# Values' upper columns as a token-major Strassen step ahead of queries and keys

## The chip, the cores and the metric

The kernel runs on one core of a Trainium2 chip. The core has a matmul engine (PE, with its weight loads shown apart as PEld), a vector engine (DVE), a scalar engine (ACT), a general engine (POOL), and a queue engine (SP) that issues nearly all DMAs in this kernel. Matmuls write to PSUM, which has eight banks of 128 partitions by 512 float32 numbers; DVE and ACT read PSUM, POOL can't. Everything else lies in SBUF, with 128 partitions. The metric is device time in microseconds of one execution, as the median of several runs.

## The reference

A block of a language model on 1024 tokens of width 1024, all in float32. Eight attention heads with a forgetting gate (512 columns) and eight groups of a gated mixing over chunks of 128 tokens (512 columns) are computed side by side from one input projection, and joined by an output projection. Then follows a gated feed-forward part of width 2816 with a short convolution. The parts that matter here:

```python
def chunked_spatial_gating(u, vg, v_gain, w_s, b_s):
    ...
    vg = rmsnorm(vg, v_gain.reshape(G, Dg))
    vc = vg.reshape(B, nc, CHUNK, G, Dg)
    w = w_s * jnp.tril(jnp.ones((CHUNK, CHUNK), dtype=w_s.dtype))
    mixed = jnp.einsum('gij,bnjgd->bnigd', w, vc) + b_s.T[None, None, :, :, None]
    return (u * mixed.reshape(B, S, G, Dg)).reshape(B, S, G * Dg)

def reference(...):
        ...
        xn = rmsnorm(h, norm_mix_g[layer])
        proj = xn @ w_in[layer]
        q = proj[..., :Q_END].reshape(B, S, N_ATT_HEADS, ATT_HEAD_DIM)
        k = proj[..., Q_END:K_END].reshape(B, S, N_ATT_HEADS, ATT_HEAD_DIM)
        v = proj[..., K_END:V_END].reshape(B, S, N_ATT_HEADS, ATT_HEAD_DIM)
        log_f = jax.nn.log_sigmoid(
            (proj[..., G_END:] + b_forget[layer]).astype(jnp.float32))
        att = forgetting_attention(q, k, v, log_f)
        uv = jax.nn.gelu(proj[..., V_END:G_END])
        ...
        sg = chunked_spatial_gating(u, vg, gmlp_norm_g[layer], w_spatial[layer], b_spatial[layer])
        mix = jnp.concatenate([att, sg], axis=-1)
        h = h + mix @ w_out[layer]
        h = h + conv_ffn(rmsnorm(h, norm_ffn_g[layer]), w_up[layer], conv_w[layer],
                         conv_b[layer], w_down[layer])
    return rmsnorm(h, norm_final_g)
```

## The kernel before

**Precision.** Each float32 operand is split into a high part and a low part of a shorter float format (`fp32r`): ACT casts the high part, DVE subtracts it from the source (`split_w`, L151). A product is then three matmuls: high by high, high by low, low by high.

**Strassen.** Large products are cut in two along the tokens, the contraction and the columns, and done with seven block products instead of eight. The blocks of x are called B11, B21, B22 and T1 to T4 (sums and differences), those of the weights A11, A12, A22 and S1 to S4. The class `Weights` (L434) loads a set, `sums` and `last_sum` form S1 to S4 on POOL, and `split` makes the two parts. `product` (L425) is one feature-major block product: 4 blocks of the contraction by 3 terms, 12 matmuls, with a block of 128 weight columns stationary and 512 tokens moving. `tmul` (L259) is token-major: a block of 128 tokens of x is stationary, and the weight's columns move; one call does 4 token blocks by 3 terms for one block of the contraction.

**Order of the stages.** First the two gate halves (u and vg), then the values' lower 256 columns together with the forget gate's 8 columns (`values_low`, `values_high`, L485, 264 moving columns). Then the queries and keys in four steps (`qk_step`, L594). A step computes 128 columns of q and of k at once, two heads of each, in seven products; `emit` (L570) scales by the norm (`rb`, the inverse root mean squares of all tokens laid along a row), splits and stores them to DRAM. Between the products the next step's weights are loaded and split (`nxt_of`, L579), and the forget gate's running sums are formed (`forget_sums`, L534), whose negative goes to DRAM, comes back, is split on POOL and stored once more (L798 to L854).

After the last step come the values' upper 256 columns, in token-major form with 256 moving columns: four products of 48 matmuls each, against T3, B11, B21 and B22, into two PSUM banks that hold 256 columns of two token blocks each (L803 to L847). This is the eight-product form, with one sum of weights on POOL (L815). `evac_v` (L684) scales the values by the norm and splits them into the tiles `V`; `kept` (L696) does this for the lower columns, which were kept in DRAM. During this stage the gate's gain and splits are also done, and head 0's operands are loaded (`head_loads`, L823). Then come the mixing (`spatial`, L744: 8 groups of three matmuls of 512 columns, bias and multiplication by u on DVE, ACT and POOL) and the turning of the gated tiles (`turn_sg`, L775, 32 transposes). Then attention starts: logits of head 0 for the row blocks 7 down to 0 (`logits_mm`, L914; `logits_min`, L924, adds the causal mask `msk` and takes the row minimum; `logits_exp`, L941), with two PSUM places for two row blocks.

**Attention** runs 40 steps of one list, 5 for each head: turning of the probabilities, products with the values, and the logits of the next head. The output projection of the gated tiles is cut in 16 pieces (`sg_out`, L996) that fill PE's waits at places that `FILLS` (L21) names.

**The end** is the down projection, also in Strassen form (`dprod`, L1529). Its last product, A22, updates the last four token blocks; each is then squared, normalized and stored (`finish`, L1606).

**What sets the order.** The program is written once, and a planner at build time orders each engine's instructions by their place in the text and by when it takes them to be ready; it also gives out the buffers, so an instruction can pass another that isn't ready. Places where it must not are tied by hand: `after` puts one instruction behind another, `seq` (L710) chains PE in attention, `behind` and `gates` hold back side work, and `act.on` and `dve.on` keep an engine in the text's order. SP executes its DMAs in order. Buffers have tags with counts (`BUFS`): for instance 4 of `raw` (loaded weights), 4 of `whl` and 2 of `wy` (split weights), 3 of `pt`, 4 each of `G`, `H` and `V`, 2 of `A`.

## Time and profile before

| what | us |
|---|---|
| median of three runs | 1055.32 |
| lowest, highest | 1055.31, 1055.50 |
| the profiled execution | 1055.89 |
| its span, first to last instruction | 1054.2 |
| end of the last query and key product | about 183.3 |
| first matmul of the mixing | 206.6 |
| first matmul of attention's logits | 215.6 |

The granted clock of PE is 0.999 over the span. A row of the timeline or of a group gives the engine, the line of the kernel, the operation, the tiles written and read, the shape, and the count. In the busy time of PE a matmul's end is modelled and lies beyond the start of the next, so a pace is read from starts. Idle time before an instruction, and what ended it, stands in brackets.

### The profile page before, as it was taken

To read this page: it belongs to the slowest core of one execution; us is meant where nothing else is said; L and a number is where in the kernel's file an instruction comes from. 1 tells how busy PE (TensorE), PEld (TensorE's weight loads), DVE (VectorE), ACT (ScalarE), POOL (GpSimd) and SP (SyncE) were. 2 spreads that over 40 slices of the span, in tenths; PEclk is the share of its full clock that TensorE was granted. 3 is DMA by queue.
4 is the path that set the end of the run, shared out by engine and by line. 5 is a ranking of instruction groups with operands and counts; after the bars stand their busy time and mean duration, and the time that the engine had idled before them with its cause. 6 is when DMAs were issued, how large, how long until landed. Compare 5 with 4: busy or idle time off the path is not lost.

```text
span 1054.2 us, 14328 instructions
## 1 busy us (share of the span) xinstructions
PE 1043.7 (99%) x5028; PEld 874.0 (83%) x5028; DVE 883.1 (84%) x1291; ACT 568.4 (54%) x1005; POOL 234.7 (22%) x177
## 2 busy tenths in 40 slices
PE   9999999999999999999999999999999999999997
PEld 7988888988888888888888888888888888888886
DVE  6898787777787769998999989899897866897774
ACT  6777544557766736654444444444444554454653
POOL 0003241420420740253333423323331000000000
PEclk9999999999999999999999999999999999999999
DMA  9623465756655444222255332331322999333442
GB/s 313 222 16 135 125 167 164 218 163 183 186 155 160 159 161 161 80 82 99 81 179 170 120 109 82 130 120 67 131 84 80 309 325 313 103 99 100 146 119 95
DMA packets 67471, 155.77 MB, mean 148 GB/s; under 512 B 9060, under 2 KB 10036, under 8 KB 67400
## 3 DMA queue, kind: packets, MB, share of 16 engines
q1 hardware_dynamic: 66088, 154.82, 46.6%
q8 instruction: 39, 0.64, 0.3%
q14 instruction: 32, 0.26, 0.1%
q10 hardware_dynamic: 1312, 0.04, 0.1%
HBM read 111.96 MB, written 42.87 MB: 147 GB/s over the span
## 4 chain that ended last, share of the span: by engine, by line
PE 90%; DVE 4%; DMA 2%; ACT 2%; issue 1%; SPq 0%; ACTq 0%; DVEq 0%
PE k L1546 20%; PE qc L1288 11%; PE qa L1288 11%; PE qd L1288 11%; PE qb L1288 5%; PE ps L265 4%; PE pb L984 3%; PE pb L968 2%; PE pb L265 2%; PE qa L430 2%; PE qc L430 2%; PE qd L430 2%; PE pl L920 1%; PE pl L921 1%; PE pf L1008 1%; PE pf L1009 1%
## 5 line engine op out<-in xcount | busy, mean ns | idle before, releaser
L1546 PE MATMUL k<-whb,wha 128*128 128x512 f32 x924 | 209.7, 389 | 0.0
L1546 PEld LDWEIGHTS k<-whb,wha 128*128 128x128 f32 x924 | 173.3, 188 | 36.2 <-DVE wha L161 0.2
L1288 PE MATMUL qc<-xT,whb 128*128 128x512 f32 x540 | 129.8, 389 | 0.2 <-ACT whb L155 0.2
L1288 PE MATMUL qa<-xB,wha 128*128 128x512 f32 x528 | 127.4, 390 | 0.0
L1288 PEld LDWEIGHTS qc<-xT,whb 128*128 128x128 f32 x540 | 101.3, 188 | 21.6 <-ACT whb L155 0.6
L1288 PEld LDWEIGHTS qa<-xB,wha 128*128 128x128 f32 x528 | 98.8, 188 | 20.9 <-DVE wha L161 0.4
L155 ACT CAST wha<-sg 128x512 fp32r<-128x512 f32 x77 | 47.8, 622 | 96.9 <-PE k L1546 84.4
L155 ACT CAST whb<-sg 128x512 fp32r<-128x512 f32 x82 | 50.5, 618 | 87.7 <-PE qc L1288 67.5
L161 DVE TENSOR_TENSOR wha<-sg,wha 128x512 fp32r<-128x512 f32 x77 | 52.8, 688 | 39.5 <-ACT wha L155 39.4
L1288 PE MATMUL qd<-xB,whb 128*128 128x512 f32 x264 | 63.7, 389 | 0.0
L1288 PE MATMUL qd<-xT,whb 128*128 128x512 f32 x264 | 63.7, 389 | 0.0
L969 ACT CAST pt<-pb 128x512 fp32r<-128x512 f32 x72 | 40.5, 585 | 41.5 <-PE pb L968 36.1
L1172 POOL TENSOR_TENSOR sg<-raw 128x512 f32<-128x512 f32 x20 | 31.1, 1555 | 139.1 <-DVE whb L161 79.9
L1288 PE MATMUL qb<-xT,whb 128*128 128x512 f32 x252 | 61.0, 389 | 0.0
L161 DVE TENSOR_TENSOR whb<-sg,whb 128x512 fp32r<-128x512 f32 x82 | 57.0, 697 | 4.4 <-ACT whb L155 4.3
L970 DVE TENSOR_TENSOR pt<-pb,pt 128x512 fp32r<-128x512 f32 x72 | 47.9, 688 | 15.1 <-ACT pt L969 14.9
L1288 PEld LDWEIGHTS qd<-xT,whb 128*128 128x128 f32 x264 | 49.5, 188 | 10.5 <-DVE u L1395 0.3
L1288 PEld LDWEIGHTS qd<-xB,whb 128*128 128x128 f32 x264 | 49.6, 188 | 10.3
L1288 PEld LDWEIGHTS qb<-xT,whb 128*128 128x128 f32 x252 | 47.2, 188 | 10.0 <-DVE whb L161 0.3
L984 PE MATMUL pb<-pt,V 128*128 128x512 f32 (+3 forms) x192 | 49.6, 362 | 0.4 <-DVE pt L970 0.3
L1175 POOL TENSOR_TENSOR sg<-sg,raw 128x512 f32<-128x512 f32 x20 | 33.4, 1672 | 63.3 <-DVE whb L161 63.3
L1173 POOL TENSOR_TENSOR sg<-sg,raw 128x512 f32<-128x512 f32 x20 | 35.1, 1754 | 47.2 <-issue 44.6
(412 smaller groups left out, 2269.8 us busy)
## 6 DMA issues: line engine op xcount, KB each, us to landing
raw<-wup SPq DMA_DIRECT2D x44, 512.0 KB
sg<-hx SPq DMA_DIRECT2D x77, 256.0 KB
hx<-hs SPq DMA_DIRECT2D x44, 256.0 KB
hx<-ca SPq DMA_DIRECT2D x35, 256.0 KB
xT<-wdn SPq DMA_DIRECT2D x28, 256.0 KB
x<-kd SPq DMA_DIRECT2D x24, 256.0 KB
A<-xtok SPq DMA_DIRECT2D x8, 512.0 KB
raw<-wqk SPq DMA_DIRECT2D x8, 512.0 KB
```

Of the source, the lines that this page charges most:

```text
L155: act.copy(h, src)
L161: return eng.tensor_tensor(out=l, in0=src, in1=f32(h), op=ALU.subtract)
L265: pe.matmul(banks[m], xs(n, xi, k)[:, ms], w[:, wi, :], start=(first and k == 0 and c == 0 and (own or m % 2 == 0)), stop=(k == 3 and c == ...
L430: pe.matmul(ps, w[:, wi, ks], xs(n, xi, k), start=(first and c == 0), stop=(c == 11), skip_group_check=True)
L969: casts.append(act.copy(pt[:, 0, :], ptr))
L970: los.append(dve.tensor_tensor(out=pt[:, 1, :], in0=ptr, in1=f32(pt[:, 0, :]), op=ALU.subtract))
L984: seq(pe.matmul(po[half][:, o:o + w], lhs, pt[:, s, c:c + w], start=(new and s == 0), stop=(s == 1 and (half, k) in ((1, 6), (0, 3))), ski ...
L1172: pool.tensor_tensor(out=s[0], in0=a21, in1=a22, op=ALU.add)
L1173: pool.tensor_tensor(out=s[1], in0=s[0], in1=a11, op=ALU.add)
L1175: pool.tensor_tensor(out=s[3], in0=s[1], in1=a12, op=ALU.add)
L1288: pe.matmul(ps, w[:, wi, ks], xb[:, xi, k, :], start=(first and n == 0), stop=(n == 11), skip_group_check=True)
L1546: pe.matmul(banks[bk + m], xh[:, xi, ms], wh[:, wi, :], start=(first and p_ == 0 and n == 0), stop=(p_ == NP - 1 and n == 2), skip_group_c ...
```

## The change

The values' upper columns are done before the queries and keys, as one Strassen step with a set of weights of its own (`Weights(4)`, the values' columns laid out like those of a step). Its seven products are token-major (`vproduct`): a block of 128 tokens is stationary, 128 weight columns move, and the four token blocks of a PSUM bank are done in turn. The four result blocks are combined on DVE and stored to a DRAM tensor `vu`. They come back into one tile when attention is at its third step, and are scaled and split in the steps 5 to 12, one token block in each.

The gate's gain and splits move in among these products, and so do the spatial weights and the forget gate's sums, whose negative is now split at once, without the round trip. Mixing follows the first product of step 0 of the queries and keys. Its low part lies in other tiles, so one matmul of 512 columns becomes two of 256. The gated tiles are turned inside the steps 1 to 3. In step 3 the tiles for q, k and two of the weights are taken from other tags; the first output weights and head 0 are loaded there, and the lower values of the first half are scaled and split there. Attention then starts right after step 3 and `kept(1)`. The mask is written into the buffer of `rb`. Of the places of `FILLS` one moves from head 0's first step to the start. Three warming matmuls at the start go, the first product is done by pairs of token blocks, and the last product of the end is cut for its last token block at column 320, into a bank of its own, so that its parts are squared apart.

```diff
 NFF = 22
-WARM = 11
-
-FILLS = {(-1, j): 1 for j in (5, 3, 2)} | {(h, s): 1 for h in range(6) for s in ((0, 2, 4) if h == 0 else (2, 4))}
+WARM = 8
+
+FILLS = {(-1, j): 1 for j in (5, 3, 2, 0)} | {(h, s): 1 for h in range(6) for s in (2, 4)}
 FCFG = ("b", 4, 4)
...
-        for m, c in sorted(ops, key=lambda o: (o[1] > 0, o)) if apart else ops:
+        for m, c in sorted(ops, key=lambda o: (o[0] // 2, o[1])) if apart else ops:
...
     values_high(1)
-    W = [Weights(0)]
-    W[0].split("A11")
+    wv = Weights(4)
+    wv.split("A11")
     values_high(2)
-    W[0].split("A12")
-    W[0].sums()
-    W[0].last_sum()
+    wv.split("A12")
+    wv.sums()
+    wv.last_sum()
     values_high(3)
     gates["high"] = newest[0]
...
     gate_norm()
+    gain = sb("pt", [P, 512])
+    sp.dma_start(out=gain, in_=ggain.to_broadcast((P, 512)))
     xu = {}
+
+    def vproduct(ps, w, n, first):
+        for k in range(4):
+            for c, (xi, wi) in enumerate(((0, 0), (0, 1), (1, 0))):
+                for m in range(4):
+                    ms = slice(m * P, (m + 1) * P)
+                    pe.matmul(ps[:, ms], xs(n, xi, k)[:, ms], w[:, wi, k * P:(k + 1) * P],
+                              start=(first and k == 0 and c == 0 and m == 0), stop=(k == 3 and c == 2),
+                              skip_group_check=True)
 
     def q1(i, tag):
         qa = psq(tag)
...
         act.copy(xu[i][:, 0, :], qa)
         return qa
-
-    qa = q1(0, "a")
-    q2 = psq("a")
-    product(q2, W[0].w["A12"], "B21", True)
 
     def forget():
 
...
-        sp.dma_start(out=ncr.rearrange("h (t p) -> (h t) p", p=P), in_=rows)
+        pool.tensor_copy(hi_, rows)
+        pool.tensor_tensor(out=lo_.bitcast(F32R), in0=rows, in1=f32(hi_), op=ALU.subtract)
+        for n, t in ((0, f32(hi_)), (1, lo_)):
+            sp.dma_start(out=ncd[n].rearrange("h (t p) -> (h t) p", p=P), in_=t)
         yield
 
+    def gate_gain(hf):
+        for t in (0, 2):
+            v = vgt[hf][:, t:t + 2, :]
+            dve.tensor_tensor(out=v, in0=v, in1=gain.unsqueeze(1).to_broadcast((P, 2, 512)), op=ALU.mult)
...
+    def gate_split(hf, gh):
+
+        if vgh[gh] is None:
+            vgh[gh] = sb("G", [P, 4, 8, 64], F32R)
+        if hf:
+            l = lw[gh]
+        else:
+            if gh == 0:
+                vgl[0] = sb("G", [P, 8, 4, 64], F32R)
+            l = vgl[0][:, gh * 4:gh * 4 + 4]
+        src = vgt[hf][:, :, gh * 256:(gh + 1) * 256].rearrange("p t (g d) -> p g t d", g=4)
+        h = vgh[gh][:, :, hf * 4:hf * 4 + 4, :]
+        act.copy(h, src)
+        dve.tensor_tensor(out=l, in0=src, in1=f32(h), op=ALU.subtract)
...
+    def spatial():
+
+        tmp = [sb("raw", [P, 4, 256]) for _ in range(2)]
+        v3 = lambda t: t.rearrange("p (t d) -> p t d", d=64)
+        for g in range(8):
+            ps = bank()
+            gs = slice(g * 64, (g + 1) * 64)
+            vh_ = vgh[g // 4][:, g % 4]
+            pe.matmul(ps, ws[0][:, g, :], vh_, start=True, stop=False)
+            for hf, vl_ in ((0, vgl[0][:, g]), (1, lw[g // 4][:, g % 4])):
+                pe.matmul(ps[:, hf * 256:hf * 256 + 256], ws[0][:, g, :], vl_,
+                          start=False, stop=False, skip_group_check=True)
+            pe.matmul(ps, ws[1][:, g, :], vh_, start=False, stop=True)
+            u = [ut[hf][:, :, gs] for hf in range(2)]
+            dve.scalar_tensor_tensor(out=u[0], in0=v3(ps[:, 0:256]), scalar=bs[:, g:g + 1], in1=u[0],
+                                     op0=ALU.add, op1=ALU.mult)
+            t = tmp[g // 4][:, g % 4, :]
+            act.activation(t, ps[:, 256:512], AF.Identity, bias=bs[:, g:g + 1])
+            pool.tensor_tensor(out=u[1], in0=v3(t), in1=u[1], op=ALU.mult)
...
+    va, v2 = psq("a"), psq("a")
+    vproduct(va, wv.w["A11"], "B11", True)
+    vx = sb("pt", [P, 2, 512])
+    x1, u2 = vx[:, 0, :], vx[:, 1, :]
+    act.copy(x1, va)
+    vproduct(v2, wv.w["A12"], "B21", True)
+    wv.split("S2", "S3")
     fg = forget()
+    fsum = forget_sums(*fg)
+    next(fsum)
+    gate_gain(1)
+    next(fsum)
+    gate_gain(0)
+    ws = spatial_weights()
+    rtags[0] = ("whl",) * 4
+    lw = [sb("wy", [P, 4, 4, 64], F32R) for _ in range(2)]
+    wv.split("S1")
+    W = [Weights(0)]
+    vb = psq("b")
+    vproduct(vb, wv.w["S2"], "T2", True)
+    dve.tensor_tensor(out=u2, in0=vb, in1=x1, op=ALU.subtract)
+    wv.split("A22")
+    vc = psq("c")
+    vproduct(vc, wv.w["S3"], "T3", True)
+    vr = ring(F32)
+    r22, r12 = vr[:, 0, :], vr[:, 1, :]
+    dve.tensor_tensor(out=r22, in0=u2, in1=vc, op=ALU.add)
+    gate_split(1, 0)
+    gate_split(1, 1)
+    vd_ = psq("d")
+    vproduct(vd_, wv.w["S1"], "T1", True)
+    next(fsum)
+    dve.tensor_tensor(out=r22, in0=r22, in1=vd_, op=ALU.subtract)
+    dve.tensor_tensor(out=x1, in0=v2, in1=x1, op=ALU.add)
+    W[0].split("A11")
+    wv.split("S4")
+    gate_split(0, 0)
+    vproduct(vc, wv.w["A22"], "T4", False)
+    dve.tensor_tensor(out=r12, in0=u2, in1=vc, op=ALU.add)
+    gate_split(0, 1)
+    W[0].split("A12")
+    W[0].sums()
+    W[0].last_sum()
+    vproduct(vd_, wv.w["S4"], "B22", False)
+    dve.tensor_tensor(out=u2, in0=vd_, in1=u2, op=ALU.subtract)
+    for r_, h_, f_ in ((x1, 0, 0), (r12, 0, 1), (u2, 1, 0), (r22, 1, 1)):
+        sp.dma_start(out=vu[4 * h_:4 * h_ + 4, :, f_ * P:(f_ + 1) * P].rearrange("m p f -> p m f"),
+                     in_=r_.rearrange("p (m f) -> p m f", f=P))
+    qa = q1(0, "a")
+    next(fsum)
+    spatial()
+    rtags[0] = RTAG
+    q2 = psq("a")
+    product(q2, W[0].w["A12"], "B21", True)
+    W[0].split("S2", "S3")
...
+        tq_, tk_ = global_ if i < 3 else (sb("H", [P, 2, 1024]), sb("H", [P, 2, 1024]))
...
+            late_w = sb("V", [P, 2, 2, 512], F32R)
+
+            def wsplit(n, j):
+                w.w[n] = late_w[:, j]
+                split_w(w.src[n], (late_w[:, j, 0], late_w[:, j, 1]))
+        else:
+            def wsplit(n, j):
+                w.split(n)
+        wsplit("S1", 0)
+        if i > 0:
...
+        if i == 3:
+            wrs.extend(sg_load(0))
+            head_loads(0)
+        if i in (1, 2):
+            turn_sg(0, i - 1)
+        elif i == 3:
+            turn_sg(0, 2)
+            turn_sg(0, 3)
...
+        if i in (1, 2):
+            turn_sg(1, i - 1)
+        elif i == 3:
+            turn_sg(1, 2)
+            turn_sg(1, 3)
+            for k in range(2, 4):
+                whs.append(sg_split(wrs[k]))
+            kept(0)
+        next(nxt)
...
+    idr = rb
+    msk = idr[:, 0:512].bitcast(BF16)
+    pool.memset(msk[:, 0:1024 - P], 0.0)
+    pool.tensor_copy(msk[:, 1024 - P:1024], maskb)
...
     for j in (7, 6):
-        logits_mm(0, j, firsts[j])
...
+        logits_exp(0, j, logits_min(0, j, logits_mm(0, j, firsts[j])))
+    for j in range(5, -1, -1):
...
+        if n == 2:
+            vh = sb("A", [P, 8, 256])
+            sp.dma_start(out=vh, in_=vu.rearrange("t p f -> p t f"))
+        if 5 <= n < 13:
+            evac_v(n - 5, 1, vh[:, n - 5, :])
...
+        if cut:
+            taken()
         for m in range(4):
+            if cut and m == 3:
+                for ps, o in ((banks[m], slice(0, cut)), (banks[bk + m], slice(cut, 512))):
+                    for r in rest:
+                        step(m, *r, ps, o)
+                continue
...
+    CUT = 320
...
+            a, b = slice(0, CUT), slice(CUT, 512)
+            less(m, banks[m], a)
+            act.activation(x3[m][:, a], y[4 + m][:, a], AF.Square, accum_out=ssa)
+            d = less(m, banks[4 + m], b)
+            act.activation(x3[m][:, b], y[4 + m][:, b], AF.Square, accum_out=r)
+            after(tc, dve.scalar_tensor_tensor(out=b_, in0=ssa, scalar=1.0 / 1024, in1=b_,
+                                               op0=ALU.mult, op1=ALU.add), d)
...
-    wv1 = kh[:, :, :, 1280:1536].transpose(1, 2, 0, 3)
 
     qk = w_in[:, :1024].reshape(2, 4, P, 2, 4, P).transpose(4, 2, 3, 0, 1, 5)[:, :, ::-1].reshape(4, P, 4, 512)
+    vu = kh[:, :, :, 1280:1536].reshape(2, 4, P, 2, P).transpose(2, 3, 0, 1, 4)[:, ::-1].reshape(1, P, 4, 512)
+    qk = np.concatenate([qk, vu])
```

More of the change, by code (lines that the diff above doesn't have):

```diff
@@ L686, in evac_v @@
         p3 = ps.rearrange("p (h d) -> p h d", h=4)
[L687 to L699 removed]
+        act.activation(v[:, :, 0, :], p3, AF.Copy, scale=rstd1[:, tt:tt + 1])
@@ L705, in block_kernel @@
-    kept(0)
-    sgT = [None] * 4
-    order = []
-    def seq(m):
-        if order:
-            after(tc, m, order[0])
-        order[:] = [m]
-    queued = []
-    def sg_load(hf):
-        wrs = []
-        for kp in range(2):
-            wr = sb("raw", [P, 2, 512])
-            queued[:] = [sp.dma_start(out=wr, in_=wos[hf, kp])]
-            after(tc, queued[0], loads[0])
-            wrs += [wr[:, 0, :], wr[:, 1, :]]
-        return wrs
-    splits = []
-    def sg_split(wr, hi="act"):
-        w = sb("whl", [P, 2, 512], F32R)
-        splits[:] = [split_w(wr, (w[:, 0], w[:, 1]), hi, "pool")]
-        return w
@@ L821, in block_kernel @@
     abs_, places = [None] * 8, {}
+    heads = []
     def head_loads(h):
+        if not heads:
+            heads.extend(sb("x2", [P, 2, 1024], F32R) for _ in range(2))
+        a2s, b2s = heads
         ab = sb("x1", [P, 2, 1024], F32R)
@@ L871, in block_kernel, with seq @@
+    for i in range(4):
+        qa = qk_step(i, qa, nxt_of(i))
+    kept(1)
+    head_loads(1)
+    a2s, b2s = heads
+    order = []
+    def seq(m):
+        if order:
+            after(tc, m, order[0])
+        order[:] = [m]
+    idr = rb
+    msk = idr[:, 0:512].bitcast(BF16)
+    pool.memset(msk[:, 0:1024 - P], 0.0)
+    pool.tensor_copy(msk[:, 1024 - P:1024], maskb)
     attT = [None] * 4
```

340 lines of the change are left out of this document (115 added, 225 removed).

## The prediction

> **What bounds the kernel now.** I read the page first, then its chain of waits, then the matmul groups with their shapes kept apart, then stretches of the timeline.
>
> ```profile
> span 1054.2 us, 14328 instructions
> PE 1043.7 (99%) x5028; PEld 874.0 (83%) x5028; DVE 883.1 (84%) x1291; ACT 568.4 (54%) x1005; POOL 234.7 (22%) x177
> PEclk9999999999999999999999999999999999999999
> PE 90%; DVE 4%; DMA 2%; ACT 2%; issue 1%; SPq 0%; ACTq 0%; DVEq 0%
> ```
>
> The matmul engine is never short of work, holds its full clock in every slice, and carries nine tenths of the chain that ends last. So every slot added to it or taken from it is time, and other engines count only where they make it wait. There are as many weight loads as matmuls (x5028 both): no matmul reuses the weights of the one before.
>
> A busy matmul engine says nothing about the pace, so the next view is the pace by shape. The end of a matmul is modelled and overlaps the next; the slot is (busy minus one duration) over (count minus one).
>
> ```profile
> L1546 PE MATMUL k<-whb,wha 128*128 128x512 f32 x924 | 209.7, 389 | 0.0
> ...
> L265 PE MATMUL ps<-whl,x 128*128 128x256 f32 x96 | 12.1, 284 | 0.1
> ...
> L265 PE MATMUL ps<-whl,V 128*128 128x256 f32 x48 | 5.9, 283 | 0.0
> L265 PE MATMUL ps<-whl,t 128*128 128x256 f32 x48 | 5.9, 283 | 0.0
> ```
>
> A matmul with 512 moving columns takes (209.7 - 0.389) / 923 = 0.227 us, one with 256 takes (5.9 - 0.283) / 47 = 0.120 us. The three lower rows are the values' upper columns: 96 + 48 + 48 = 192 matmuls, 192 x 0.120 = 23.0 us.
>
> ```profile
> 183.50:207.00 23.50, 23.38 (x193) 23.14 (x192) 18.57 (x32) 11.75 (x26) 8.38 (x8) 1.00 0.78 212
> ```
>
> This is a row of busy time by stretch (stretch, length, then PE, weight loads, DVE, ACT, POOL with counts, clock, DMA share, GB/s), cut to that stage: 23.38 of 23.50 us of matmuls, 23.14 of weight loads, so nearly no stall to win there.
>
> **Values' upper columns.** The step replaces 192 matmuls by seven products of 48: 4 k-blocks, 3 hi/lo terms, 4 token blocks, each with only 128 moving columns, since tokens are the stationary side and the output is half of 256 columns. That is 336 matmuls. In columns streamed it is 336 x 128 against 192 x 256, an eighth less. But each has a weight load of its own. What does a matmul cost when it is shorter than its load? The forget gate's sums have the only run of several short ones, with 64 moving columns:
>
> ```profile
> 120.02 0.28 PE L553 MATMUL pb<-gg 128*128 128x64 f32 x1
> 120.10 0.19 PEld L552 LDWEIGHTS pb<-gg 128*128 128x128 f32 x1
> 120.13 0.28 PE L552 MATMUL pb<-gg 128*128 128x64 f32 x1
> ...
> 120.22 0.19 PEld L553 LDWEIGHTS pb<-gg 128*128 128x128 f32 x1
> 120.24 0.28 PE L553 MATMUL pb<-gg 128*128 128x64 f32 x1
> 120.33 0.30 PEld L430 LDWEIGHTS qc<-V,whl 128*128 128x128 f32 x2
> 120.36 0.48 PE L430 MATMUL qc<-V,whl 128*128 128x512 f32 x1
> ```
>
> Starts at 120.02, 120.13, 120.24 and 120.36: 0.11 us apart, and so are the loads (120.10, 120.22, 120.33), though 64 columns are half of 128. The load sets this pace, not the columns. Against it stands a pair of 128-column matmuls in attention:
>
> ```profile
> 284.21 0.22 PE L920 MATMUL pl<-x 128*128 128x128 f32 x1
> 284.21 0.19 PEld L921 LDWEIGHTS pl<-x,x 66*128 66x128 f32 x1
> 284.27 0.28 PE L921 MATMUL pl<-x,x 66*128 66x128 f32 x1
> ```
>
> The second starts 0.06 us after the first. There the load of the first came under a long matmul ahead of both, so one load is saved up; a run of 48 has none to save up. Bounds: 336 x 0.06 = 20.2 us, if every matmul ran as that second one; and 336 x 0.120 = 40.3 us, since a 128-column matmul with one load can't outlast a 256-column one with one load. I take 0.111, the pace of the run: 336 x 0.111 = 37.3 us, **+14.3 us** (bounds -2.8 and +17.3).
>
> The Trainium skill, page "TensorE: Matmul & The Clock Gate", section "Back-to-back issue gap", gives about 81 ns for each matmul of a sustained stream of load and matmul pairs at 128 columns. By that figure the step would be 336 x 0.081 = 27.2 us, +4.2 us (an estimate from the page); the run above, with its 0.11, goes against it.
>
> Is the other work of that stage hidden under 37.3 us? It carries the gate's gain, its splits, five weight splits and two of the first query/key step, six combinations of 128x512 and the spatial weights' split.
>
> ```profile
> L44 DVE TENSOR_TENSOR G<-G,gms 128x1024 f32<-128x1024 f32 x4 | 4.6, 1219 | 0.0
> L44 DVE TENSOR_TENSOR whl<-raw,whl 128x512 fp32r<-128x512 f32 x5 | 3.3, 687 | 1.9 <-ACT whl L44 1.9
> ```
>
> The first row has the shape of a gain (4 of 1.22) and nearly that of a gate split (4 of 1.22) or the spatial weights' (1); the second that of the weight splits and combinations (13 of 0.69). 9 x 1.22 + 13 x 0.69 = 20 us of DVE: hidden, at nothing. Without cover a weight split would cost its 0.69. The step's DMAs: the weights are 1 MB as before; four stores of 256 KB and later one load of 1 MB come new, the small round trip of the negated sums goes. The stores wait on SP for the last combination; behind them wait the next weights' loads and the stores of q and k, which have a step of seven products, 84 x 0.227 = 19 us, to spare. The first query product's copy on ACT needs the buffer that two of these stores read. If ACT stood still until they land, at the 212 GB/s of that stage's row 1 MB takes 4.9 us, of which the product covers 12 x 0.227 = 2.7: bounds 0 and 2.2, and I take nothing, as ACT has other ready work and PE four free banks. The new weights' sums go to POOL, idle for 15 of the 23.5 us above.
>
> **Mixing.** Per group one matmul of 512 becomes two of 256: 8 x (2 x 0.120 - 0.227) = **+0.1 us**. It sits between two products, as do the 32 transposes, whose count is unchanged.
>
> **Moved stalls.** Two of today's waits stand at places that vanish or change, as does the start of attention:
>
> ```profile
> 182.27 1.07 PE L430 MATMUL qd<-t,wy 128*128 128x512 f32 x4
> 186.44 0.19 PEld L265 LDWEIGHTS ps<-whl,x 128*128 128x128 f32 x1 [0.32 <-DVE whl L44]
> 186.92 0.68 DVE L44 TENSOR_TENSOR G<-G 128x512 f32<-128x512 f32 x1
> ...
> 216.85 1.28 DVE L51 CUSTOM_DVE_ANT_0 t<-pl,t,lim 128x1024 f32<-128x1024 f32 x1 [0.76 <-PE pl L921]
> 218.20 0.50 PE L920 MATMUL pl<-x 128*128 128x512 f32 x1 [0.57 <-DVE mn L51]
> ```
>
> ```profile
> L796 POOL COPY t<-maskb 128x128 bf16<-128x128 bf16 x1 | 3.4, 3378 | 0.0
> ```
>
> (The last row is from the groups by line, the others from the timeline.) 0.32 + 0.57 = 0.9 us of waits go. But the last query product ends near 183.3 while DVE ends that step's work at 187.6, 4.3 us late; today the values' matmuls cover it. In the new order the first logits follow at once: rows 7 and 6 are eight matmuls (six of 512, two of 384 columns), about 1.7 us, then PE waits for the first minimum (1.28 us), which waits for DVE and for a mask that POOL now writes into the buffer of rstd (memset, then the copy of 3.4 us) after its readers. If DVE finishes its work first: 4.3 + 1.3 - 1.7 = 3.9 us of waiting; with the mask written only after the last reader of rstd, three DVE operations (0.68 each), a memset, the copy, the minimum and less the 1.7, about 6. If the planner puts the minimum ahead, nothing. I take 2, so **+1.1 us** net (bounds -0.9 and +5.1). The fill moved to this place follows the wait and can't cover it.
>
> The upper values' scaling moves into heads 1 and 2, one of each per step:
>
> ```profile
> L51 DVE SCALAR_TENSOR_TENSOR V<-ps,rstd,V 128x256 fp32r<-128x256 f32 x4 | 1.9, 484 | 1.8 <-ACT V L51 1.7
> ```
>
> ```profile
> 272.00:291.00 19.00, 18.83 (x112) 16.25 (x111) 15.28 (x32) 13.49 (x30) 5.91 (x6) 1.00 0.65 183
> ```
>
> Eight of 0.484 on DVE, and as many of ACT's half. In the stretch of the second row, about a head, DVE is busy 15.28 of 19.00 us, so each fits into idle time; at its place it may push a split that PE waits for. Bounds 0 and 8 x 0.484 = 3.9; **+0.3 us**, near the lower, as the head's PE stalls are 19.00 - 18.83 in all.
>
> **The ends.** At the start three warming matmuls of 11 go:
>
> ```profile
> 1.29 4.88 PE L122 MATMUL ps<-gg 128*128 128x512 bf16 x11 [1.29 <-DVE pad L133]
> ...
> 7.33 2.44 PE L265 MATMUL pb<-wy,V 128*128 128x512 f32 x10
> 8.49 0.69 DVE L51 TENSOR_TENSOR wy<-raw,wy 128x512 fp32r<-128x512 f32 x1
> ```
>
> They are about 0.43 apart, so the first product could begin 1.3 us sooner; at that slow pace of the first microseconds this is worth three slots, 0.7 us. But the second k-block's low weights come at 8.49 + 0.69 = 9.18, and the matmul that needs them first is the last of the ten in the second row, at about 9.4: most is lost there again. **-0.1 us** (bounds -0.7, 0). The end:
>
> ```profile
> 1047.42 0.69 DVE L1646 TENSOR_TENSOR y<-y,k 128x512 f32<-128x512 f32 x1 [0.49 <-PE k L1546]
> ...
> 1048.14 0.63 ACT L1647 ACTIVATE xB<-y 128x512 f32<-128x512 f32 x1 [0.52 <-DVE y L1646]
> ```
>
> The last 512 columns are cut at 320. Nine matmuls become nine of 320 and nine of 192: by slots (0.227 - 0.120) / 256 a column, 9 x (0.147 + 0.111 - 0.227) = +0.3 us. The last subtraction and square then have 192 columns; from 0.69 to about 0.43 and 0.63 to 0.44 by the 256-column rows' 0.48, and the last matmul itself is some 0.1 shorter: **-0.2 us** in sum (bounds -0.5, +0.3).
>
> **Sum.** 14.3 + 0.1 + 1.1 + 0.3 - 0.1 - 0.2 = +15.5 us. The profiled execution took 1055.89 us with a span of 1054.2; the median of the runs shown is 1055.32 (they span 1055.31 to 1055.5). The difference belongs on the median: 1070.8 us; the next profile's span about 1069.7.
>
> **Rivals.** *Full column pace* (not slower). If the engine saves up loads throughout, the matmuls run at the 0.06 of the pair: 20.2 - 23.0 = -2.8, with the +1.2 of the rest 1053.7. It decides where the mean slot is below (23.0 - 1.2) / 336 = 0.065 us. For: the pair. Against: four short ones in a row at 0.11. Chance 0.06.
>
> *Every other load hidden.* Slots of 0.06 and 0.111 in turn, mean 0.0855: 28.7 us, +5.7, +1.2: 1062.2. For: the pair is just this pattern. Against: the run of four shows no short slot. The Trainium skill's 81 ns (the section named above) stands beside this mean. Chance 0.08.
>
> *A late start of attention* (slower still). DVE's backlog and the mask hold the first minimum to the full bound: +4.0 above my value, and the evacuations displace splits by 2: 1076.8. For: DVE's 4.3 us lag and the 3.4 us copy. Against: the tk half of that lag is over sooner when its mask region is free, and the planner may order it so. Chance 0.14.
>
> *The change doesn't do what it says*: the number of matmuls is written out in its loops; I give this nothing.
>
> **How the numbers follow.** The forecast, 1068 to 1074 with its own bounds, has 0.72. The range of 8 in 10 reaches to the second rival below and over the third above: 1062 to 1078. Only the first rival lies near or under 1055.3; a measurement of this kernel tells 0.2%, 2.1 us, from no change. Of its 0.06 about 0.04 is faster, 0.02 the same; slower has 0.94.
>
> **What would show it.** Right: the 336 matmuls of the step stand 0.11 us apart, loads busy throughout while matmul columns are half idle; the stage is 37 us long and attention starts about 14 us later. One row with the mean slot decides it; 0.06 or 0.086 proves me wrong. The wait ahead of the third logits row shows the second term. Wrong in another way: gaps inside the seven products (a split or sum late), or a clock below full there.

## The result

The changed kernel takes 1080.13 us in the median of four runs (1079.75 to 1080.51), beside 1055.41 for the kernel before (1055.31 to 1055.66). The ratio is 1.0234, with a 95% interval from 1.0216 to 1.0252: 24.7 us slower. The sign was predicted, the size was not: 1070.8, and the range ended at 1078. The profiled execution took 1080.05 us with a span of 1078.3, 24.1 more than the span before. One execution of one experiment, the scaling of the kept values behind the sixth row, took 2445.32 us and stays out of its median.

The page of the changed kernel:

```profile
span 1078.3 us, 14654 instructions
PE 1061.1 (98%) x5186; PEld 890.3 (83%) x5186; DVE 889.0 (82%) x1294; ACT 570.0 (53%) x1005; POOL 235.3 (22%) x176
PEclk9999999999999999999999999999999999999999
PE 92%; DVE 2%; ACT 2%; POOL 1%; issue 1%; DMA 1%; SPq 0%; ACTq 0%; POOLq 0%; DVEq 0%
```

TensorE still carries the chain that ended last (92%), but its busy share of the span fell from 99 to 98%: there is more work, and there are new waits. Forty slices hide where. Busy time by stage (stretch, length, PE, weight loads, DVE, ACT, POOL with counts, clock, DMA share, GB/s) of the changed kernel shows it:

```profile
105.80:143.40 37.60, 37.60 (x340) 37.60 (x338) 21.88 (x38) 13.53 (x22) 4.35 (x2) 1.00 0.16 51
143.40:153.20 9.80, 9.03 (x50) 7.47 (x50) 4.36 (x7) 4.09 (x10) 5.37 (x8) 1.00 0.13 33
153.20:167.00 13.80, 11.01 (x49) 8.78 (x47) 7.82 (x13) 4.63 (x9) 8.62 (x9) 1.00 0.48 152
167.00:186.00 19.00, 18.95 (x85) 15.71 (x86) 16.50 (x24) 8.31 (x15) 6.80 (x4) 1.00 0.60 164
...
224.00:238.40 14.40, 11.59 (x57) 9.21 (x55) 13.03 (x24) 6.95 (x15) 1.08 (x2) 0.97 0.69 176
238.40:255.00 16.60, 16.55 (x66) 13.65 (x67) 6.32 (x17) 6.62 (x16) 0.00 (x0) 0.82 0.83 237
```

The first row is the values' upper columns: no idle time, loads busy throughout, 37.6 us where the stage before took 23. In the second, third and fifth row shown PE is idle for 0.8, 2.8 and 2.8 us, and in the last row the clock is at 0.82.

**The first new wait** is in step 0 of the queries and keys (timeline of the changed kernel; in brackets the idle time before an instruction and what ended it):

```profile
153.13 4.90 POOL L628 TENSOR_TENSOR A<-raw,A 128x256 f32<-128x256 f32 x5
...
161.89 1.28 POOL L453 TENSOR_TENSOR raw<-raw,raw 128x512 f32<-128x512 f32 x1 [3.85 <-DMA raw<-wqk]
...
165.22 1.09 DVE L44 TENSOR_TENSOR whl<-gg,whl 128x512 fp32r<-128x512 f32 x1 [3.94 <-ACT whl L44]
...
166.23 0.67 DVE L44 TENSOR_TENSOR G<-pt,qc 128x512 f32<-128x512 f32 x1
...
167.06 1.16 PE L431 MATMUL qc<-V,whl 128*128 128x512 f32 x4 [2.84 <-DVE G L44]
```

Read from below. TensorE waits 2.84 us for a subtraction on DVE. That stands in DVE's order behind the split of a sum of the next step's weights, which waits for POOL's sums, and these wait for the weights' load. The load was late because it had no buffer: two of the four `raw` buffers are the mixing's `tmp` tiles, read by POOL until 158.03. SP's own waits say so (us in total, times, longest):

```profile
SPq L440 <- POOL A L628: 5.8, 1, 5.8
SPq L441 <- POOL A L628: 3.3, 1, 3.3
```

The mixing itself stalls too, since POOL's sums of the first weights run among its multiplies. ACT, which has to empty PSUM for the mixing, first waits for one of these sums. (The first row is a group by line, and its last column is idle time before it; the second is from the timeline.)

```profile
L618 PE MATMUL pb<-G,pt 128*128 128x512 f32 x8 | 3.3, 419 | 0.8 <-ACT raw L44 0.8
151.30 0.62 ACT L44 CAST whl<-gg 128x512 fp32r<-128x512 f32 x1 [1.48 <-POOL gg L454]
```

**The second** is the start of attention (timeline of the changed kernel):

```profile
235.44 0.62 ACT L44 CAST H<-H 128x512 fp32r<-128x512 f32 x1 [2.22 <-DVE H L44]
235.54 0.34 PE L913 MATMUL pl<-x,x 66*128 66x384 f32 x1
236.12 0.68 DVE L44 TENSOR_TENSOR H<-H 128x512 f32<-128x512 f32 x1
236.72 0.47 DVE L44 SCALAR_TENSOR_TENSOR V<-pt,rstd,V 128x256 fp32r<-128x256 f32 x1
...
237.11 1.27 DVE L44 CUSTOM_DVE_ANT_0 t<-pl,t,lim 128x1024 f32<-128x1024 f32 x1
...
238.45 0.80 PE L912 MATMUL pl<-x 128*128 128x512 f32 x1 [2.58 <-DVE mn L44]
...
239.90 0.63 PE L1000 MATMUL pf<-whl,G 128*128 128x512 f32 x1
...
240.33 0.63 PE L1001 MATMUL pf<-whl,G 128*128 128x512 f32 x1
```

DVE is still scaling and splitting the last queries (`H`) and the kept values (`V`) when the first rows of logits are done; the first minimum begins at 237.11. Then comes something that no term of the prediction held: matmuls of 512 columns now start 0.43 us apart (239.90, 240.33), not 0.227. The stretches of the same execution give the clock:

```profile
235.50:238.40 2.90, 0.37 (x3) 0.06 (x1) 2.90 (x7) 0.56 (x1) 0.00 (x0) 0.83 0.92 244
238.40:242.00 3.60, 3.55 (x9) 2.91 (x10) 2.09 (x4) 3.06 (x5) 0.00 (x0) 0.50 0.93 265
242.00:244.40 2.40, 2.40 (x7) 1.88 (x6) 0.00 (x0) 0.23 (x2) 0.00 (x0) 0.53 0.99 300
244.40:248.00 3.60, 3.60 (x18) 2.98 (x18) 1.56 (x4) 1.55 (x4) 0.00 (x0) 1.00 1.04 246
```

For some 6 us behind the idle stretch TensorE is busy at half clock; some 13 matmuls that each start 0.2 us late make 2.6 us lost. The page's slices, all nines, show nothing of it.

### The profile page after: what moved, and what is told of

Same layout as the page of the kernel before. It is cut to its first block, busy times and chain, and to the rows that moved or that the text cites. A ratio compares the mean times of both kernels' runs of the same rounds, so it can differ in the third digit from the quotient of the medians.

```text
span 1078.3 us, 14654 instructions
## 1 busy us (share of the span) xinstructions
PE 1061.1 (98%) x5186; PEld 890.3 (83%) x5186; DVE 889.0 (82%) x1294; ACT 570.0 (53%) x1005; POOL 235.3 (22%) x176
## 4 chain that ended last, share of the span: by engine, by line
PE 92%; DVE 2%; ACT 2%; POOL 1%; issue 1%; DMA 1%; SPq 0%; ACTq 0%; POOLq 0%; DVEq 0%
PE k L1528 19%; PE qc L1268 11%; PE qa L1268 11%; PE qd L1268 11%; PE qb L1268 5%; PE pb L266 5%; PE ps L266 4%; PE pb L976 2%; PE pb L960 2%; PE qa L431 2%; PE qc L431 2%; PE qd L431 2%; PE pf L1000 1%; PE pl L912 1%; PE pl L913 1%; PE pf L1001 1%
## 5 line engine op out<-in xcount | busy, mean ns | idle before, releaser
L1528 PE MATMUL k<-whb,wha 128*128 128x512 f32 (+2 forms) x933 | 210.0, 387 | 0.0
L44 DVE TENSOR_TENSOR pt<-pb,pt 128x512 fp32r<-128x512 f32 (+1 forms) x84 | 55.8, 686 | 19.3 <-ACT pt L44 13.3
L44 DVE SCALAR_TENSOR_TENSOR cg<-h,cp,cg 128x1023 f32<-128x1023 f32 (+1 forms) x44 | 66.8, 1517 | 4.8 <-ACT cg L44 4.4
L44 DVE SCALAR_TENSOR_TENSOR ca<-h,cp,ca 128x1023 f32<-128x1023 f32 (+1 forms) x44 | 67.2, 1528 | 3.7 <-ACT ca L44 3.7
```

Source lines behind the costliest of these rows:

```text
L44: r = f(*args, **kw)
L1528: pe.matmul((banks[bk + m] if ps is None else ps)[:, o], xh[:, xi, ms], wh[:, wi, o], start=((first and p_ == 0 or new) and n == 0), stop= ...
```

## The experiments

Each edit is made on the changed kernel unless it says otherwise, and differences are taken from its 1080.13 us. A median is of four executions where no other number is given. The kernel before, timed beside each group of edits, had medians between 1055.1 and 1055.4, and the ratios are to it.

### What sets the pace of the seven products

Token blocks outside the terms (one execution):

```diff
-            for c, (xi, wi) in enumerate(...):
-                for m in range(4):
+            for m in range(4):
+                for c, (xi, wi) in enumerate(...):
```

> The seven products with the loop over the four token blocks outside the loop over the three terms, so that three matmuls in a row add into the same 128 columns, two of them with the same 128x128 of x; 336 matmuls as before. If each matmul pays its own weight load, nothing changes: starts 0.111 to 0.112 us apart, products 5.36 us, stage 37.6 us, time 1080. If the pace comes from jumping between the four column blocks of a bank at each matmul, or if repeated weights are kept, the slot falls toward 0.06 to 0.09 us and the stage to 20 to 30 us, time 1063 to 1073.

1080.69 us. The products are the same, 48 matmuls in 5.5 us:

```profile
L518 PE MATMUL qb<-wy,H 128*128 128x128 f32 x48 | 5.5, 275 | 0.0
```

(5.5 - 0.275) / 47 = 0.111. The order in which the four column blocks of a bank are written is not the cause, and nothing is won where two matmuls in a row have the same 128x128 of x.

Each matmul of 128 columns as two of 64, each with a load (one execution):

```diff
-  pe.matmul(ps[:, ms], ..., w[:, wi, k * P:(k + 1) * P])
+  for o in (0, 64):
+      pe.matmul(ps[:, m * P + o:m * P + o + 64], ..., w[:, wi, k * P + o:k * P + o + 64])
```

> Each matmul of the seven products is split into two with 64 moving columns: the same columns streamed, twice the weight loads (672). If the load sets the pace, each of the 672 takes 0.111 us again: products 10.7 us, stage about 75 us, time about 1117. If the moving columns set it, each takes about half, 0.056 us: stage and time as they are, 37.6 and 1080. In between (a fixed cost per matmul of 0.03 beside the columns): 0.08 us each, stage 54.

1183.97 us, where 1117 was expected if the load sets the pace: a miss in size, for a reason worth the run. Stretches of this kernel:

```profile
105.96:110.00 4.04, 4.04 (x37) 4.04 (x36) 4.04 (x9) 1.53 (x7) 0.00 (x0) 0.95 0.35 134
110.00:112.00 2.00, 2.00 (x11) 2.00 (x11) 2.00 (x3) 1.98 (x2) 0.00 (x0) 0.50 0.02 4
...
120.00:135.00 15.00, 15.00 (x72) 15.00 (x72) 1.23 (x1) 1.53 (x2) 0.00 (x0) 0.50 0.00 0
```

In the first row 37 matmuls take 4.04 us, 0.11 each: half the columns at the same pace, so the pace is set by what each pair of load and matmul pays once. I take that for the load; another fixed cost of a pair would look the same here. Then the clock falls to half and stays there, though PE and its loads are busy all the time; 72 in 15 us are 0.21 each. With 128 columns at 0.11 us the clock stays at 1.00 (the first stage row above).

Features on the stationary side, as in the steps of queries and keys: 84 matmuls of 512 columns, and 16 transposes in attention.

```diff
-    def vproduct(ps, w, n, first):
-        ...
+    vproduct = product
...
-            evac_v(n - 5, 1, vh[:, n - 5, :])
+            pv = bank()
+            for f_ in range(2):
+                seq(pe.transpose(pv[:, f_ * P:(f_ + 1) * P], vh[:, tt // 4 * 2 + f_, tt % 4 * P:(tt % 4 + 1) * P], ident))
+            evac_v(tt, 1, pv[:, 0:256])
```

> The seven products turned over: 128 weight columns stationary and 512 tokens moving, as in the query and key steps, so 84 weight loads in place of 336 for the same multiplications; the result blocks are turned back to token rows by 16 transposes in attention's steps 5 to 12. If the loads are the price, the seven products fall from 37.5 to 7 x 2.72 = 19.0 us of matmuls, 16 x 0.11 = 1.8 us come back, and the time falls by 14 to 17 us to 1063 to 1066; DVE has 21.9 us of work in the stage, so up to 4 us of it may turn into waits (1067). If the long stage were set by DVE or by the place and not by the loads, the time stays above 1075.

1064.48 us, ratio 1.0084 (1.0068 to 1.0101): 15.7 less. 336 x 0.111 - 84 x 0.227 - 16 x 0.11 = 16.5 was at stake. The main term is shown.

### The wait in step 0

The mixing's second half on DVE straight from PSUM, with no `tmp`:

```diff
-        tmp = [sb("raw", [P, 4, 256]) for _ in range(2)]
...
-            act.activation(t, ps[:, 256:512], AF.Identity, bias=bs[:, g:g + 1])
-            pool.tensor_tensor(out=u[1], in0=v3(t), in1=u[1], op=ALU.mult)
+            dve.scalar_tensor_tensor(out=u[1], in0=v3(ps[:, 256:512]), scalar=bs[:, g:g + 1], in1=u[1],
+                                     op0=ALU.add, op1=ALU.mult)
```

> Mixing's second half is added and multiplied on DVE straight from PSUM like the first half, instead of ACT, two tiles of the loaded weights' buffers and POOL. If the 3.0 us wait in step 0 and the 0.9 us wait within mixing come from these two buffers (held until POOL has multiplied) and from POOL, both vanish: -3 to -4 us, 1076 to 1077; DVE takes 8 x 0.48 = 3.9 us more where it is idle half the time. If the wait of step 0 comes from the order of DVE alone or from the weights' sums, it stays and the time is 1079 to 1082.

1074.84 us, ratio 1.0184 (1.0169 to 1.0199): 5.3 less. Its stretches from the mixing to the end of step 0's wait, where PE was idle for 0.8 and 2.8 us:

```profile
143.00:153.20 10.20, 10.20 (x59) 8.79 (x59) 6.18 (x15) 3.54 (x7) 3.34 (x4) 1.00 0.12 32
153.20:168.00 14.80, 14.80 (x67) 12.26 (x66) 11.95 (x21) 4.05 (x7) 4.80 (x4) 1.00 0.27 81
```

Both waits are gone, so the way the mixing's second half was done was their cause. The edit takes away the two buffers, POOL's multiplies and ACT's copies together; which of them caused which wait is read from the rows above and was not tried apart.

The rest of the gain lies in the clock, as far as the two profiled executions show it. At the start of attention, where this edit changes nothing, its stretches are:

```profile
236.00:238.00 2.00, 2.00 (x6) 1.63 (x5) 0.59 (x2) 1.71 (x4) 0.00 (x0) 0.50 0.86 227
238.00:240.00 2.00, 2.00 (x8) 1.55 (x8) 0.00 (x0) 0.00 (x0) 0.00 (x0) 0.74 1.03 324
```

The half clock lasts 3.4 us in this execution (235.61 to 239.03), and 6.8 us in the changed kernel's (237.44 to 244.26). By the starts of the matmuls, 1.1 us less are lost behind the wait. With the 3.6 us of waits that is 4.7, and the spans of the two profiles differ by 4.6 (1078.3 and 1073.7).

### The start of attention

The scaling of the kept values behind the sixth logits row:

```diff
-    kept(1)
     head_loads(1)
...
         fill((-1, j))
+        if j == 2:
+            kept(1)
```

> The scaling and splitting of the second half of the lower values (four of 0.48 us on DVE, four on ACT) is written behind the logits of row 2 of head 0 instead of ahead of the first logits; nothing else. If DVE's backlog of the last query and key step holds up the first row minimum, the wait ahead of the third logits row falls from 2.7 us by up to 1.9 us, PE is then idle too briefly for its clock to fall, and the half-clock stretch behind it (2.6 us) goes too: -3.5 to -5 us, 1075 to 1076.5. If the mask on POOL or the loads of head 0 hold it up, the wait and the time stay, 1079.5 to 1080.5.

A miss: 1084.15 us in the median of three executions, ratio 1.0274, some 4 us slower. The wait stayed, at 2.4 us instead of 2.6, since DVE still did the last queries' evacuation ahead of the first minimum. And 1.6 us were lost anew among the first turnings (starts at 254.87 and 256.60), where TensorE waited for DVE. With the mixing's edit as well:

> Both edits in one kernel: mixing's second half on DVE, and the second half of the lower values behind the first logits. If the two waits are separate, the gains add: -5.3 and -3.5 to -5, so 1069.5 to 1071.5. If one only moves the other's wait, the sum is short by 2 us or more: above 1073.

1076.39 us (1075.55 to 1079.35), 1.6 more than with the mixing's edit alone (1073.61 to 1075.82); and with both that and the feature-major products:

> The feature-major products with the two edits on the waits. If load pace, buffers and DVE's backlog are all there is, the gains add to the time of the turned-over products: 1064.5 - 5.3 - 4.3 = 1054.9, with 1.5 either way, about the time of the kernel before. If the shorter stage uncovers DVE's 21.9 us of work, it ends at 1057 to 1061.

1060.82 us, ratio 1.0047 (1.003 to 1.0064), and not the 1054.9 of plain addition.

Then the last evacuation of queries, for heads 6 and 7, written behind the first turnings:

```diff
-        emit(tq_, qd, i, -0.125, (hi,))
+        if i < 3:
+            emit(tq_, qd, i, -0.125, (hi,))
+        else:
+            held_emit.append(lambda: emit(tq_, qd, i, -0.125, (hi,)))
```

> Step 3's last scaling, copy, subtraction and stores of q (for heads 6 and 7) are written behind the first turnings; all else is the changed kernel. Theory (DVE comes late to the first minimum because of step 3's last evacuations, the copy on ACT between two of them above all): the first minimum begins at about 235.7 instead of 237.1, the wait ahead of the third logits row falls from 2.7 to about 1.2 us, the clock keeps its full speed and no matmul of the logits is 0.43 us apart: 1.5 + 2.6 = 4 us less, 1076 us. Rival A (kept columns' scaling or the mask hold it as well): under 1 us less, 1079 to 1080, the wait stays above 2 us. Rival B (the wait moves to the turnings): the first wait goes but the stretch from 250 to 260 gets as much longer, 1079 to 1081.

1084.92 us, slower by 4.8. DVE's timeline says why:

```profile
235.57 0.68 DVE L44 SCALAR_TENSOR_TENSOR H<-H,t 128x512 f32<-128x512 f32 x1
236.93 0.69 DVE L44 TENSOR_TENSOR H<-H 128x512 f32<-128x512 f32 x1 [0.68 <-ACT H L44]
237.54 1.28 DVE L44 CUSTOM_DVE_ANT_0 t<-pl,t,lim 128x1024 f32<-128x1024 f32 x1
```

The two operations on `H` are still ahead of the minimum. They now stand behind all the scalings of `V` (235.57 instead of 234.72), and the minimum begins later, 4.4 us behind the first logits instead of 3.7. The wait grew from 2.6 to some 3.3 us, and TensorE lost another 3 us between 256 and 294. The order of an engine is planned here, not taken from the text, and the edit did not bring the evacuation behind the minimum, as it was meant to. So a tie to the latest row minimum (the evacuation then stands behind row 2 in the text too):

```diff
+            if mins:
+                after(tc, x, mins[-1])
```

> As the version with the emit written later, and now its first scaling is tied behind the minimum of the sixth logits row (row 2), so that VectorE's order has all but the last two minima ahead of it; the kept columns' scaling stays. Theory (VectorE reaches the first minimum late because this evacuation, with its copy on ScalarE, stands ahead): the first minimum begins at about 235.7 instead of 237.1, the wait falls from 2.7 to about 1.2 us, and no matmul after it is 0.43 us apart: 4 us less, 1076 us. Rival A (the wait is bound by the kept columns and the turned tiles alike): the wait stays above 2 us and the half clock with it, 1079 us or more. Rival B (what is moved stands in the way of the first turnings): the wait goes, but the stretch from 250 to 260 takes it back, 1079 to 1082.

The timeline of DVE, then the stretches of the tied kernel:

```profile
234.04 1.66 DVE L44 SCALAR_TENSOR_TENSOR V<-pt,rstd,V 128x256 fp32r<-128x256 f32 x4
235.62 1.28 DVE L44 CUSTOM_DVE_ANT_0 t<-pl,t,lim 128x1024 f32<-128x1024 f32 x1
```

```profile
235.00:236.00 1.00, 0.45 (x3) 0.13 (x1) 1.00 (x3) 0.00 (x0) 0.00 (x0) 1.00 1.00 186
236.00:237.00 1.00, 0.04 (x1) 0.04 (x1) 1.00 (x3) 0.06 (x1) 0.00 (x0) 0.83 0.96 272
237.00:238.00 1.00, 1.00 (x3) 0.81 (x4) 0.97 (x2) 1.00 (x2) 0.00 (x0) 0.50 0.87 272
...
280.00:290.00 10.00, 9.34 (x55) 7.92 (x54) 9.95 (x23) 7.21 (x17) 0.00 (x0) 1.00 0.62 164
290.00:300.00 10.00, 9.13 (x51) 7.50 (x50) 7.82 (x15) 8.09 (x18) 8.31 (x8) 1.00 0.87 293
```

The minimum begins at 235.62, as expected, and the wait is 1.5 us. Yet half clock follows all the same, and with DVE's new order PE is idle for 1.5 us of the last two rows, where the changed kernel has 0.1: 1082.34 us, ratio 1.026 (1.0244 to 1.0277). Taking this work from in front of the minimum did not pay in any of the three forms.

Instead TensorE can be kept busy. First with 26 idle transposes of the identity into a bank that nobody reads:

```diff
+    dummy = bank()
+    for c in range(26):
+        seq(pe.transpose(dummy[:, c % 4 * P:(c % 4 + 1) * P], ident, ident))
     for j in range(5, -1, -1):
```

> 26 transposes of the identity, 0.11 us each, into a PSUM bank that nobody reads, are put on PE between the first two rows of logits and the third: PE has work in the wait and the wait itself stays 2.7 to 3.0 us. If the half clock behind the wait is the consequence of PE's idleness, it is gone: the 13 matmuls at 0.43 us take 0.227, -2.4 to -2.8 us, 1077.3 to 1077.8. If the clock falls for another reason (what went before, or a fixed time), it falls here too and the time stays at 1080 or is up to 0.3 us longer.

1079.0 us, ratio 1.0226 (1.0211 to 1.0241). Stretches of this kernel:

```profile
236.00:238.00 2.00, 2.00 (x18) 1.88 (x17) 2.00 (x5) 0.34 (x1) 0.00 (x0) 1.00 0.89 274
238.00:240.00 2.00, 2.00 (x11) 1.67 (x10) 1.72 (x4) 2.00 (x5) 0.00 (x0) 1.00 0.86 269
```

The minimum comes no sooner (3.66 us behind the first logits in both), but in this execution, of 1077.86 us, the clock stays full: the half clock was a consequence of idleness. The other profiles bear this out. Half clock follows at the start of attention in all twelve where TensorE waits there for 1.5 us or more, and in none of the three where it has work there instead. Yet the median is only 1.1 us lower, and not the 2.4 to 2.8 expected: the executions of 1079.93 and 1080.86 us had a granted clock of 0.997 instead of 0.999, and no profile shows where it fell in them.

Then with useful work, the first of the fills (12 matmuls of the output projection) ahead of the third row:

```diff
+    fill((-1, 5))
     for j in range(5, -1, -1):
         logits(0, j)
-        fill((-1, j))
+        if j < 5:
+            fill((-1, j))
```

> The first of the four fills between the logits rows (12 matmuls of the output projection) stands ahead of the third logits row (row 5) instead of behind it; all else is the changed kernel. Theory (TensorE's idle stretch there costs its own length and brings the half clock; useful work in its place saves both): the wait of 2.7 us goes to below 0.5, no matmul behind it is 0.43 us apart, 5 us less, 1075 us. Rival A (the wait only moves by one row, behind rows 5 and 4, which now follow without a fill between them): 2 us less, 1078. Rival B (the turnings behind the rows set the time, and what is won here is lost there): 1080.

A miss again, 1079.58 us and not 1075: ratio 1.0225 (1.0211 to 1.0239), four executions from 1077.22 to 1081.29. In the profiled one, of 1077.22, the start of attention is mended, but step 0 is not:

```profile
163.00:166.20 3.20, 0.74 (x4) 0.28 (x2) 1.57 (x2) 1.14 (x2) 2.17 (x2) 0.95 0.32 123
166.20:169.20 3.00, 2.74 (x7) 2.19 (x8) 2.91 (x6) 1.05 (x2) 0.00 (x0) 0.50 0.00 0
...
235.50:238.40 2.90, 2.90 (x15) 2.44 (x14) 2.90 (x7) 0.62 (x1) 0.00 (x0) 1.00 0.87 215
238.40:242.00 3.60, 3.38 (x15) 2.29 (x14) 3.59 (x7) 2.83 (x5) 0.00 (x0) 1.00 0.93 280
```

The wait at 163, there in both, is followed by half clock here and by full clock in the changed kernel's profile. The same wait costs its length, or that and 3 us at half clock, 1.5 us more. So of the some 5 us won at the start of attention the span keeps 2.8 (1078.3 to 1075.5): 1.5 go in step 0, and 0.8 in a new wait for DVE ahead of the first turning.

### The start, and the sums

The kernel before with the two edits of the start alone (`WARM = 8`, first product in pairs of banks; eleven executions):

> The kernel before, with the change's two edits of the start alone: 8 warming matmuls instead of 11, and the first products of gated tiles in pairs of banks. Theory (the trace after had the later stages begin 0.7 us sooner): 0.7 us less than before, 1054.6. Rival (the prediction's step: the second block's low weights hold it): 0.0 to 0.1 us less, 1055.2.

1055.18 beside 1055.28 us, ratio 0.9998 (0.999 to 1.0007): nothing that can be measured.

Features stationary, the mixing on DVE, and one edit at the start of attention: the evacuation written later, which lengthens the wait; the tie; the fill first (five, five and eleven executions).

> Three edits on the changed kernel: seven products with features on the stationary side, the second half of the mixing on VectorE, and the last scaling of q behind the first turnings. Theory (main term 37.6 us against 19 to 21 us, buffer wait at step 0, late first minimum, each undone by its own edit, and the sum of the parts holds): 1080.1 - 15.7 - 5.3 - 4 = 1055 us, the same as before within 2 us. Rival A (the waits slide into one another, as the version with the kept columns moved showed): 1058 to 1061. Rival B (the half clock goes in each version and adds nothing of its own): 1052 to 1054, faster than before.

> The tie, with the products that have features on the stationary side and the mixing's second half on VectorE. Theory: as the first two edits gave 15.7 and 5.3 us and the tie 4: 1055 to 1057 us, the same as before. Rival (the tie wins nothing, as in the sum without it): 1061 to 1063.

> The fill first, with features on the stationary side and the mixing's second half on VectorE. Theory: 1080.1 - 15.7 - 5.3 - 5 = 1054 to 1056 us, the same as before. Rival (as the other sums of edits showed, the start of attention gives back what it won): 1059 to 1061.

1063.41, 1060.71 and 1056.88 us. The last has the ratio 1.0014 (1.0005 to 1.0023), 23.3 of the 24.7 us undone. The first two edits without a third were not run together; by addition they give 1080.1 - 15.7 - 5.3 = 1059.1, so some 2 us are the fill's, an estimate. The page of the last:

```profile
span 1055.3 us, 14175 instructions
PE 1043.4 (99%) x4950; PEld 869.3 (82%) x4950; DVE 887.9 (84%) x1302; ACT 566.6 (54%) x997; POOL 228.5 (22%) x168
```

78 matmuls fewer than the kernel before, and no gain: TensorE's waits, the distances of starts less the slots, sum to some 14 us here and some 10 in the kernel before. No version of the changed kernel here beats the kernel before.

## Why the prediction was too low

**What bounds the kernel**: right. TensorE sets the end, and both kinds of loss, more slots and more waiting, went through to the time.

**Values' upper columns, +14.3**: right, by the run of four short matmuls of the forget gate. 336 matmuls took 37.5 us, 0.112 each, and halving their columns did not change the pace. The first two rivals fall with it (0.06 and 0.086 a slot). The Trainium skill's 81 ns for a pair of load and matmul at 128 columns ("TensorE: Matmul & The Clock Gate", "Back-to-back issue gap") is not what these fp32r operands showed: 111 ns in all seven products.

**The next weights' loads, with "a step of seven products, 84 x 0.227 = 19 us, to spare"**: this step failed first. I followed SP's queue and not the buffers that the loads go into. The mixing was priced by its matmul slots alone, +0.1, which they are; the new tiles that its second half occupies, and POOL's work between PSUM and those tiles, were not followed. Measured: 2.8 us in step 0 and 0.8 in the mixing, undone together by the mixing's edit.

**Moved stalls, +1.1**: the step with the wrong size. The place was named and so was the cause, DVE's lag. But of the bounds -0.9 and +5.1 I took a value near the middle, for no row spoke for it, and its price left out the clock. Measured from the first logits on: 3.2 us of waiting in two pieces where there were 0.8, and then 2.6 us at half clock. The mask, which I counted as part of it, was innocent: set by 233.2, its copy 0.29 us and not the 3.4 of the row I had quoted. The third rival, 1076.8 for a late start of attention, was right in its place and about DVE's lag, but had the mask for its cause too and did not know of the clock.

**The scaling in heads 1 and 2, +0.3**: too low, by about 0.5 us. From the first logits to the end the span grew by 6.3 us (838.6 to 844.9). By the starts of the same matmuls in both kernels, 5.1 of it are there when head 1 begins: 2.4 of waits, the rest the half clock. In heads 1 and 2 comes 0.8 (the logits matmuls that start at 252.81 and 289.92 us in the kernel before start at 275.78 and 313.67), and the last 0.4 in the feed-forward part, near 475 us. That the 0.8 are the scaling's was not tried alone.

**The ends, -0.1 and -0.2**: right within what can be measured. The start alone gave 0.1; from the last matmul's start to the end there are 6.84 us instead of 7.17, with 0.28 more of matmuls ahead.

In sum, by the spans: 14.5 for the products, 4.0 from there to the first logits (most of it the waits of step 0 and the mixing), 6.3 behind them, and 0.7 less up to the first of the products in this execution are 24.1.

## What to carry to other kernels

Where matmuls are shorter than their weight loads, count loads and not columns: turn the product so that the long side moves. When a stage moves, follow its buffers as well as its queues, for a tile that takes a buffer from a pool delays the next load into that pool, steps later. A wait of a microsecond or two on TensorE can cost as much again in clock, and what helped here was not to shorten it but to put independent matmuls into it: with both other losses mended this gave the best time, 1056.88 us, while alone it left the median within 0.6 us of the changed kernel's.

## What was unexpected of the hardware

- The clock fell to half behind idle stretches of 2.9 us (the changed kernel) and of 1.5 us (the tie), and behind step 0's wait of 3 us in three profiles out of nine. The Trainium skill ("TensorE: Matmul & The Clock Gate", "Part 1: The HAM clock gate (the "warmup" mystery)") puts the fall after an idle window of about 3.4 us that runs freely. That its phase is free fits the uneven outcome; all three of these stretches are shorter than its window, and here the measurements decide.
- Behind such a wait the half clock lasted 3.4 us or 6.8 us in every profile here, nothing between: 6.8 in the changed kernel and with the tie, 3.4 with the mixing's edit and in step 0 with the fill first.
- The clock also fell to half where TensorE was never idle: with 64 columns each 0.11 us, after 4 us. With 128 columns each 0.11 us it stayed full for 37 us. So a full row of loads and matmuls did not count as busy there; that the columns streamed are what counts is an inference from these two kernels.
- POOL's copy of the same 128x128 mask took 3.4 us in the kernel before and 0.29 in the changed one, and no run shows why:

```profile
232.86 0.29 POOL L861 COPY t<-maskb 128x128 bf16<-128x128 bf16 x1
```
